# Where eight in-projection weight tiles are split and stored, and when search constants and the first modulation products run

## The chip, the core and the metric

One core of a Trainium2 chip runs the whole program. The metric is the device time of an execution in microseconds. The engines are TensorE (PE: matmuls; PEld: its weight loads), VectorE (DVE), ScalarE (ACT), GpSimd (POOL) and SyncE (SP), whose queue issues nearly all DMAs here. Each engine takes its instructions in a fixed order, and waits on semaphores for the others.

## The reference

One layer of a hybrid decoder trunk on 2048 positions of width 1024, in float32. The input is normalized, scaled and shifted by a modulation vector, projected, and handed to three groups of heads whose outputs are projected back; a gated feed-forward part follows.

```python
mod = c_act @ ada_w[l] + ada_b[l]
sh1, sc1, g1, sh2, sc2, g2 = [m[:, None, :] for m in jnp.split(mod, N_MOD, axis=-1)]
h = rmsnorm(x, norm_mix_w[l]) * (1.0 + sc1) + sh1
proj = h @ w_in[l]
(hq, hf, hi, hg, sq, sk, sv, iq, ik, iw, cu) = jnp.split(proj, offsets, axis=-1)
o_a = hgrn2_mixer(hq, hf, hi, hg, lower_bounds[l], hg_onorm_w[l])
o_b = dsa_mixer(sq, sk, sv, iq, ik, iw)
o_c = conv_module(cu, cv_w[l], cv_b[l], cv_ln_w[l], cv_ln_b[l])
mix = jnp.concatenate([o_a, o_b, o_c], axis=-1) @ w_out[l]
x = x + g1 * mix
h = rmsnorm(x, norm_mlp_w[l]) * (1.0 + sc2) + sh2
x = x + g2 * (jnp.square(jax.nn.relu(h @ mlp_w1[l])) @ mlp_w2[l])
```

`hgrn2_mixer` is a gated linear recurrence in chunks; `dsa_mixer` scores keys with a light indexer (`iq`, `ik`, `iw`), keeps the best 256 keys of each query and attends to them; `conv_module` is a causal depthwise convolution with gating and a layer norm.

## The kernel before, in words

**Precision.** Every large product is made of three: an operand is split into a high part (a cast to fp32r) and a low part (what the cast left over), and high by high, high by low and low by high are summed. So each weight tile is split once: ScalarE casts the high part (`split_w`, L317), GpSimd subtracts the low part (L318), in two halves of 128 x 512.

**Blocks.** The positions go in four blocks of 512. For each block `in_norm` loads and normalizes `x`, `to_act_steps` makes eight slices (k = 0 to 7) of the transposed, modulated activations, each with a high part `ah` and a low part `al` (L281 to L288), and `in_block` runs 26 units, each a weight tile of the in-projection times the slices (`mm_T` at L424, or `n_part` at L1244 for the wide ones, which take two weight tiles). The first units are the index keys, the two index queries (`iq`), then the first head: `hf`, `hq`, `hi` (two tiles) and `hg`. These are the first eight weight tiles. The low part of slices 1, 4 and 6 is made by VectorE, that of the others by GpSimd (L288). Of the first block the first two units run slice by slice as the slices come (`first_units`), in two PSUM tiles called `at`; the third unit is the second index query.

**Weights, once from the input and then split.** The first block fetches each tile raw (512 KB, `fetch_w`, tiles `wraw`, two buffers), splits it, uses it, and then stores both parts (1 MB in four transfers) in a DRAM tile `wk_d` (`keep_w`). The later blocks fetch both parts from there (`fetch_kept`, tiles `wk`). `specs` is the list of all weight tiles in the order of use; an entry of it is raw (its pieces, and a name such as "win", whose names in `keep` are stored) or a kept one (`kept` and its number). Kept weights use the buffers of `whi` and `wlo`, and every third one those of `wraw`, by a counter over the whole program (`w_tiles`).

**Modulation.** Scale and shift for the first slices come first: `ada_half` multiplies 32 loaded tiles `adw` of 128 x 512 by the activated `c`, most on VectorE (L238, L240), some on ScalarE with a sum on GpSimd (L233, L236), sums over the partitions by small matmuls (L226), and writes `a` and `sh` (L244). The rest of the modulation, the gates and the second norm's scale and shift, is made by `ada_gen` from the second block on, in chunks of 256 columns by `ada_part` (L197, L199).

**Constants.** `late_consts` is called in the first block ahead of its second unit. It holds `search_consts` (powers, reciprocals and products of 14 columns, L472 to L491, from which the search for the 256th score starts), the convolution's taps, the recurrence's bounds and five masks `lmask`, each of two selects on GpSimd (L514, L516) and a cast on VectorE (L518).

**What sets the order.** The program's text is not the order of the instructions: a scheduler with a model of time places each instruction on its engine's queue as soon as the model has its inputs ready and the engine free, so what is written late can stand early. `high_priority` moves a few; nothing in the kernel before fixes the place of one instruction behind another beyond that. Background work (index scores, the search for the top 256, attention, convolution, recurrence, `ada`) is written in turns between the units by `step` and `half`.

Of the kernel before, what the change touches and what calls it, by code (L numbers as in the profile page):

```python
# [8 lines left out]
F32 = mybir.dt.float32  # L9
# [11 lines left out]
P = 128  # L21
# [25 lines left out]
PREP = 14  # L47
R1 = [1126, 1216, 1594]
# [30 lines left out]
def trunk(ctx, tc, x, c, ada_w, ada_b, norm_mix_w, norm_mlp_w, w_in, hg_lb_logits,  # L79
# [61 lines left out]
    def dram(shape, dt, name):  # L141
        return tc.dram_tile(shape, dt, name=name)
# [49 lines left out]
    def ada_part(pool, wtag, wbufs, acc, sec, c0, w):  # L192
        for k in range(NK):
            t = pool.tile([P, w], F32, tag=wtag, bufs=wbufs, name=nm("adw"))
            (nc.gpsimd if AQ else nc.sync).dma_start(t, ada2[k * P:(k + 1) * P, sec * D + c0:sec * D + c0 + w])
            if k == 0:
                V.tensor_scalar(acc, t, cact[:, 0:1], None, op0=OP.mult)  # L197
            else:
                V.scalar_tensor_tensor(acc, t, cact[:, k:k + 1], acc, op0=OP.mult, op1=OP.add)  # L199
            yield 1.2 * w  # L200
# [73 lines left out]

    def to_act_steps(xh, acol, bcol, ah, al, mid=None):
        for k in range(NK):
# [11 lines left out]
            (V if k in (1, 4, 6) else G).tensor_tensor(lo, tf, hi.bitcast(F32), OP.subtract)  # L288
# [40 lines left out]
    kept = []  # L329
# [74 lines left out]
    def keep_w():  # L404

        for w, sp in given:
            if sp is not None and sp[1] in keep:
                d = dram([P, 2, TB * 2], F32, f"wk_d{len(kept)}")
                kept.append(d)
                for s_, ts in enumerate(w):  # L410
                    for n, t in enumerate(ts):
                        dma(d[:, s_, n * TB:(n + 1) * TB], raw32(t).rearrange("p k m -> p (k m)"))
        given.clear()
# [343 lines left out]
    def ada_gen():  # L757
        for sec, dst in ((2, None), (4, a2), (3, sh2), (5, None)):
            for c0 in range(0, D, AW):
                acc = hp.tile([P, AW], F32, tag="ada", bufs=1, name=nm("adacc"))  # L760
                yield from ada_part(hp, "adw", AB, acc, sec, c0, AW)
# [319 lines left out]
    def in_block(b, xts, nxt):  # L1081
        act = first_units(xts) if b == 0 else to_act(xts, a1, sh1, lambda: pump("fast", rates["fast"]))
        for u, (pieces, ev, m) in enumerate(in_units):
# [6 lines left out]
            if u == 1 and b == 0:  # L1090
                late_consts()
# [73 lines left out]
    forms = [(kk, m) for _, _, kk, m in specs]  # L1165
    for b in range(1, NB):
        specs += [(kept, i, kk, m) for i, (kk, m) in enumerate(forms)]

    where = {}

    def kept_specs(key, new):

        if key not in where:
            where[key] = len(forms) + sum(len(v[1]) for v in where.values()), new
            return new
        first, old = where[key]
        return [(kept, first + i, *(sp[2:] or (NK, P))) for i, sp in enumerate(old)]
# [476 lines left out]
```

## Time and profile before

| What | us |
|---|---|
| median of 3 runs | 2881.52 |
| lowest and highest run | 2874.92, 2886.61 |
| the profiled execution | 2886.42 |
| its span, first to last instruction | 2884.7 |
| TensorE busy in the span | 2756.2 |
| VectorE, ScalarE, GpSimd busy | 1681.3, 1239.3, 1083.3 |

The profile is of one execution. Matmuls are pipelined, so the records of two of them overlap, and TensorE counts as busy also where its matmuls run at half the clock; how fast they follow one another is seen in the distance of their starts. In rows of the timeline the first number is the start in us from the span's start, the second how long the row's instructions took together, `x8` how many there are, and in brackets the idle time of the engine ahead of the row with what ended it. In rows of groups stand the count, the busy time, the mean in ns, and the idle time ahead. The first block runs from 0 to about 245 us, the second to about 500.

### The profile page before, as it was taken

The page shows a single profiled execution, that of the slowest core. Times are in us where ns is not written, and L with a number is a line of the kernel's source. Part 1 is how long each engine was busy: PE and PEld are TensorE (multiplying, and loading weights), DVE is VectorE, ACT ScalarE, POOL GpSimd, SP SyncE. Part 2 cuts the span into 40 slices and gives each one's busy share as a digit, 9 for nine tenths or more (in the row PEclk, how much of TensorE's full clock was granted, in tenths as well). Part 3 has the DMA queues.
Part 4 walks back from the last instruction along what each step waited for, and adds up shares of the span by engine and source line. Part 5 has one row for each costly group of instructions (what it writes and reads, how often), then busy time and mean ns, then how long its engine had stood idle before and what let it go on. Part 6 is the DMA issues. An engine that isn't in the chain of part 4 may idle for free.

```text
span 2884.7 us, 42781 instructions
## 1 busy us (share of the span) xinstructions
PE 2756.2 (96%) x14116; PEld 2299.5 (80%) x14116; DVE 1681.3 (58%) x3514; ACT 1239.3 (43%) x2630; POOL 1083.3 (38%) x1051
## 2 busy tenths in 40 slices
PE   6999998999999989999999999999999999999997
PEld 5888887888788777888778888787788887777776
DVE  6695687877466447665767637476762221254455
ACT  4436444533311255555455454354543332343333
POOL 7444111212100455666564222134422223345444
PEclk9999999999999999999999999999999999999999
DMA  8987676667655668989888776778867676686676
GB/s 292 293 278 242 214 229 192 215 216 251 207 179 168 228 228 273 307 280 284 279 268 303 231 229 200 217 234 261 281 217 235 205 230 197 219 285 211 227 238 207
DMA packets 428067, 688.55 MB, mean 239 GB/s; under 512 B 43383, under 2 KB 171452, under 8 KB 427836
## 3 DMA queue, kind: packets, MB, share of 16 engines
q1 hardware_dynamic: 427680, 685.67, 73.5%
q8 instruction: 112, 1.84, 0.3%
q14 instruction: 119, 0.97, 0.1%
q10 hardware_dynamic: 156, 0.07, 0.0%
HBM read 532.74 MB, written 152.84 MB: 238 GB/s over the span
## 4 chain that ended last, share of the span: by engine, by line
PE 41%; DMA 6%; DVE 3%; POOL 1%; issue 1%; ACT 0%; SPq 0%; POOLq 0%; DVEq 0%; ACTq 0%
PE mm L1268 11%; PE ax L424 9%; PE mm L424 6%; PE ax L1268 5%; PE mm L1429 4%; PE at L929 1%; PE po L963 1%; DMA wk<-wk_d 1%; PE at L951 1%; DMA tr<-in_mlp_w_dram 1%; PE ix L809 1%; POOL wk L376 1%; DVE cum L881 1%; DMA x_d<-x 1%; DMA wk_d<-whi 1%
## 5 line engine op out<-in xcount | busy, mean ns | idle before, releaser
L424 PE MATMUL mm<-ah,wk 128*128 128x512 f32 x1728 | 461.0, 398 | 4.9 <-ACT tf L286 1.9
L424 PEld LDWEIGHTS mm<-ah,wk 128*128 128x128 f32 x1728 | 319.5, 189 | 71.1 <-ACT tf L286 2.1
L318 POOL TENSOR_TENSOR wlo<-wraw,whi 128x512 fp32r<-128x512 f32 x210 | 288.4, 1395 | 219.9 <-ACT whi L317 137.5
L961 POOL TENSOR_TENSOR pT<-L,pT 128x512 fp32r<-128x512 f32 (+3 forms) x160 | 191.0, 1195 | 387.6 <-ACT pT L960 212.1
L816 DVE SCALAR_TENSOR_TENSOR s<-r,iw_s,s 128x512 f32<-128x512 f32 (+3 forms) x266 | 236.3, 888 | 115.0 <-ACT r L811 108.4
L424 PE MATMUL mm<-al,wk 128*128 128x512 f32 x864 | 237.4, 396 | 0.0
L424 PE MATMUL ax<-ah,wk 128*128 128x512 f32 x912 | 234.5, 391 | 1.4 <-ACT hc L1403 1.4
L1268 PE MATMUL mm<-wk,hh 128*128 128x512 f32 x736 | 224.3, 396 | 3.9 <-DMA wk<-wk_d 3.5
L931 DVE CUSTOM_DVE_ANT_0 L<-at,bias 128x512 f32<-128x512 f32 (+3 forms) x152 | 93.6, 619 | 189.0 <-PE at L929 133.9
L424 PEld LDWEIGHTS ax<-ah,wk 128*128 128x128 f32 x912 | 169.5, 188 | 36.1 <-ACT hc L1403 1.8
L811 ACT ACTIVATE r<-ix 128x512 f32<-128x512 f32 (+3 forms) x256 | 134.3, 554 | 146.3 <-PE ix L809 112.5
L317 ACT CAST whi<-wraw 128x512 fp32r<-128x512 f32 x210 | 122.0, 619 | 173.0 <-DMA wraw<-in_mlp_w_dram 42.1
L273 POOL TENSOR_TENSOR hl<-hr,hh 128x512 fp32r<-128x512 f32 x96 | 131.1, 1366 | 159.8 <-ACT hh L265 159.6
L424 PEld LDWEIGHTS mm<-al,wk 128*128 128x128 f32 x864 | 161.2, 189 | 32.2
L589 DVE SCALAR_TENSOR_TENSOR cx<-hc,cvc,cx 128x512 f32<-128x512 f32 x232 | 173.8, 749 | 2.0
L881 DVE TENSOR_SCALAR_CACHE_REDUCE cum<-s,ssm 128x384 bf16<-128x384 f32 (+13 forms) x112 | 165.2, 1475 | 8.7 <-POOL s L820 6.8
L1268 PEld LDWEIGHTS mm<-wk,hh 128*128 128x128 f32 x736 | 135.5, 188 | 32.6 <-DMA wk<-wk_d 5.8
L959 ACT COPY L<-at 128x512 f32<-128x512 f32 (+3 forms) x160 | 82.7, 522 | 182.1 <-PE at L951 180.4
L1542 DVE TENSOR_TENSOR acc<-acc,mm 128x512 f32<-128x512 f32 x120 | 81.0, 683 | 125.0 <-PE mm L1268 124.4
L1429 PE MATMUL mm<-wk,hc 128*128 128x512 f32 x588 | 144.9, 392 | 6.8 <-DVE acc L1437 6.7
L945 ACT ACTIVATE L<-L,nmx 128x512 f32<-128x512 f32 (+3 forms) x160 | 103.8, 651 | 80.3 <-DVE nmx L940 79.9
L1429 PEld LDWEIGHTS mm<-wk,hc 128*128 128x128 f32 x588 | 109.5, 188 | 33.8 <-DVE acc L1437 10.5
(368 smaller groups left out, 6128.8 us busy)
## 6 DMA issues: line engine op xcount, KB each, us to landing
wk<-wk_d SPq DMA_DIRECT2D x776, 256.0 KB
wk<-wk_d SPq DMA_DIRECT2D x196, 512.0 KB
wk_d<-whi SPq DMA_DIRECT2D x210, 256.0 KB
wk_d<-wlo SPq DMA_DIRECT2D x210, 256.0 KB
wraw<-in_mlp_w_dram SPq DMA_DIRECT2D x68, 512.0 KB
kc<-sk_d SPq DMA_DIRECT2D x112, 256.0 KB
vc<-v_d SPq DMA_DIRECT2D x112, 256.0 KB
adw<-in_ada_w_dram SPq DMA_DIRECT2D x128, 128.0 KB
```

The source lines that it names most:

```text
L273: e.tensor_tensor(lo[:, i:j], src[:, i:j], hi[:, i:j].bitcast(F32), OP.subtract)
L317: A.copy(hi, src)
L318: G.tensor_tensor(lo, src, hi.bitcast(F32), OP.subtract)
L424: T.matmul(ps, ww[k], aa[k], start=(n == 0 and k0 == 0), stop=(n == len(order) - 1 and k1 == NK))
L589: V.scalar_tensor_tensor(acc if w < TAPS - 1 else total, hc[:, w:w + TB], cvc[:, m, w:w + 1], acc, op0=OP.mult, op1=OP.add)
L811: A.activation(r[:, :w], ps[:, :w], AF.Relu, scale=32.0 ** -0.5)
L816: V.scalar_tensor_tensor(s[:, c0:c0 + w], r[:, :w], iw, s[:, c0:c0 + w], op0=OP.mult, op1=OP.add)
L881: V.tensor_scalar(dump, s, t, -AIM - i * STEP, op0=OP.is_ge, op1=OP.add, accum_out=d)
L945: A.activation(lt[:, :w], lt[:, :w], AF.Exp, bias=nmx, accum_out=sm[:, cb:cb + 1])
L961: G.tensor_tensor(pT[:, :nt, 1], lv, pT[:, :nt, 0].bitcast(F32), OP.subtract)
L1268: T.matmul(ps, aa[f][:, tok * P:(tok + 1) * P], ww[i], start=(first and n == 0), stop=(last and n == 5))
L1429: T.matmul(bank[t], aa[:, k, t * P:(t + 1) * P], ww[k], start=(i in (0, 2, 4) and n == 0), stop=(n == 5), skip_group_check=True)
```

## The change

Two things are changed. **The weights:** the first eight tiles are used by the first block as before but not stored ("once" is no name in `keep`). The second block fetches these eight raw again, splits them, and stores them; the third and fourth fetch them from there. `numbers` keeps each kept tile's number as it was. Nothing else about a tile's use changes. **The order:** `lows` collects the low slices' instructions in the order written. `late_consts` stands under an edge behind the eighth (`lows[NK - 1]`, the first block's slice 7, on GpSimd), and the first chunk of `ada_gen` behind the seventh (`lows[NK - 2]`, the first block's slice 6, on VectorE). Such an edge orders only instructions on that same engine: GpSimd's instructions of `late_consts`, and VectorE's products of the first 256 columns of the first gate. DMAs and other engines are held only through what they read.

```diff
+LATE = 8
...
-    def ada_part(pool, wtag, wbufs, acc, sec, c0, w):
+    def ada_part(pool, wtag, wbufs, acc, sec, c0, w, behind=None):
...
-            if k == 0:
-                V.tensor_scalar(acc, t, cact[:, 0:1], None, op0=OP.mult)
-            else:
-                V.scalar_tensor_tensor(acc, t, cact[:, k:k + 1], acc, op0=OP.mult, op1=OP.add)
+            with tc.issue_after(behind) if behind is not None else ExitStack():
+                if k == 0:
+                    V.tensor_scalar(acc, t, cact[:, 0:1], None, op0=OP.mult)
+                else:
+                    V.scalar_tensor_tensor(acc, t, cact[:, k:k + 1], acc, op0=OP.mult, op1=OP.add)
...
+    lows = []
...
-            (V if k in (1, 4, 6) else G).tensor_tensor(lo, tf, hi.bitcast(F32), OP.subtract)
+            lows.append((V if k in (1, 4, 6) else G).tensor_tensor(lo, tf, hi.bitcast(F32), OP.subtract))
...
-    kept = []
+    kept = {}
+    numbers = []
...
-                d = dram([P, 2, TB * 2], F32, f"wk_d{len(kept)}")
-                kept.append(d)
+                i = numbers.pop(0) if numbers else len(kept)
+                kept[i] = d = dram([P, 2, TB * 2], F32, f"wk_d{i}")
...
-                yield from ada_part(hp, "adw", AB, acc, sec, c0, AW)
+                yield from ada_part(hp, "adw", AB, acc, sec, c0, AW, lows[NK - 2].ins if (sec, c0) == (2, 0) else None)
...
             if u == 1 and b == 0:
-                late_consts()
+                with tc.issue_after(lows[NK - 1].ins):
+                    late_consts()
...
+    raws = specs[:LATE]
+    specs[:LATE] = [(sp[0], "once", *sp[2:]) for sp in raws]
+    firsts = len(specs)
     for b in range(1, NB):
         specs += [(kept, i, kk, m) for i, (kk, m) in enumerate(forms)]
+    specs[firsts:firsts + LATE] = raws
...
+    numbers += [*range(LATE, len(forms)), *range(LATE)]
...
+            numbers.extend(range(where[key][0], where[key][0] + len(new)))
```

Since the scheduler's model sees other inputs ready at other times, the order changes on all engines and in most of the program. Three places are shown. Lines of the changed kernel are 1 to 12 above those before (L288 becomes L292, L318 L322, L479 L484).

GpSimd's queue from the first block's last modulation sum on, before. `al` is a slice's low part, `wlo` a weight's, `sconst` the search constants, `rs` the norm of the next block's `x`:

```order
L236 TENSOR_TENSOR adw_469<-adw_469,adw_472 128x512
L288 TENSOR_TENSOR al_368<-tf_369,ah_367 128x512
L479 TENSOR_TENSOR sconst<-sconst 128x14
L480 TENSOR_TENSOR sconst<-sconst 128x14
L318 TENSOR_TENSOR wlo_407<-wraw_373,whi_406 128x512
L318 TENSOR_TENSOR wlo_411<-wraw_373,whi_410 128x512
L288 TENSOR_TENSOR al_517<-tf_518,ah_516 128x512
L288 TENSOR_TENSOR al_539<-tf_540,ah_538 128x512
```

The same place now, as far as the fourth unit's weight (`wraw_404`):

```order
L322 TENSOR_TENSOR wlo_411<-wraw_373,whi_410 128x512
L292 TENSOR_TENSOR al_517<-tf_518,ah_516 128x512
L292 TENSOR_TENSOR al_539<-tf_540,ah_538 128x512
L477 IOTA sint 128x14
...
L519 AFFINE_SELECT mwork<-mwork 128x256
L256 TENSOR_SCALAR rs_2265<-ss_2263 128x1
...
L484 TENSOR_TENSOR sconst<-sconst 128x14
L485 TENSOR_TENSOR sconst<-sconst 128x14
...
L521 AFFINE_SELECT mwork<-mwork 128x256
L257 TENSOR_TENSOR rs_2265<-rs_2265,nhalf 128x1
...
L257 TENSOR_TENSOR rs_2274<-rs_2274,nhalf 128x1
L322 TENSOR_TENSOR wlo_644<-wraw_404,whi_643 128x512
```

The two powers (`sconst`) have moved from ahead of the sixth slice's low part to behind the eighth's, and stand with two mask selects and the norms ahead of the fourth unit's low weights; the other mask selects, which stood among the first 34 rows, follow further on.

VectorE's queue from `al_528`, the seventh low slice, to the low part `slo` of the second index query, now; `adacc` is the first chunk of `ada_gen`, `kst` the index keys:

```order
L292 TENSOR_TENSOR al_528<-tf_529,ah_527 128x512
L199 TENSOR_SCALAR adacc_3685<-adw_3686,cact 128x256
L201 SCALAR_TENSOR_TENSOR adacc_3685<-adw_3713,cact,adacc_3685 128x256
...
L478 CAST sconst<-sint 128x14
...
L201 SCALAR_TENSOR_TENSOR adacc_3685<-adw_3841,cact,adacc_3685 128x256
...
L201 SCALAR_TENSOR_TENSOR adacc_3685<-adw_4038,cact,adacc_3685 128x256
L488 RECIPROCAL sconst<-sconst 128x14
L530 TENSOR_TENSOR kst_570<-stg_568,kst_570 32x512
L543 TENSOR_TENSOR slo_636<-at_414,shi_635 128x512
L486 TENSOR_TENSOR zq<-sconst 128x14
...
L492 TENSOR_TENSOR sconst<-sconst 128x14
L543 TENSOR_TENSOR slo_677<-mm_651,shi_676 128x512
```

Before, the chunk's first four products and the constants down to the one that is now L492 stood ahead of `al_528`, among the slices; only the chunk's last four stood behind it. SP's queue at the same place now, with the loads of the index products (`ki`, `qi`) and of the raw weights of `hi`:

```order
L108 DMA iq_d_75<-slo_636 128x512
L108 DMA ki_729<-ki_d_87 96x384
L108 DMA iq_d_75<-shi_676 128x512
L108 DMA iq_d_75<-slo_677 128x512
L108 DMA qi_724<-iq_d_75 32x8x128 x3
L108 DMA wraw_682<-in_w_in_dram 128x4x256
L108 DMA wraw_751<-in_w_in_dram 128x4x256
```

and TensorE's, where these products are used:

```order
L429 MATMUL mm_761<-al_528,whi_688 128x512
L429 MATMUL mm_761<-al_539,whi_688 128x512
L814 MATMUL at_731<-ki_729,qi_724 128x384
L814 MATMUL at_736<-ki_729,qi_724 128x384
L429 MATMUL mm_692<-ah_334,wlo_644 128x512
```

Before, the first index product stood behind all products of `hi`, and the low half of each unit directly behind its high half; now two index products stand between the high halves of the fourth and fifth unit (`mm_692`, `mm_761`) and their low halves.

GpSimd's queue around the start of the second block, now; before, it had no `wlo` here:

```order
L322 TENSOR_TENSOR wlo_2888<-wraw_2783,whi_2887 128x512
L966 TENSOR_TENSOR pT_2732<-L_2719,pT_2732 128x3x128
L322 TENSOR_TENSOR wlo_3140<-wraw_2881,whi_3139 128x512
...
L322 TENSOR_TENSOR wlo_3144<-wraw_2881,whi_3143 128x512
...
L292 TENSOR_TENSOR al_3024<-tf_3025,ah_3023 128x512
...
L292 TENSOR_TENSOR al_3123<-tf_3124,ah_3122 128x512
...
L322 TENSOR_TENSOR wlo_3286<-wraw_3137,whi_3285 128x512
...
L322 TENSOR_TENSOR wlo_3290<-wraw_3137,whi_3289 128x512
...
L322 TENSOR_TENSOR wlo_3536<-wraw_3283,whi_3535 128x512
```

The first two tiles are split ahead of the second block's slices (`al_3024` is the first), the third and the following ones behind them.

## The prediction

> **What bounds the kernel now.** I read the page's busy table first, then busy time by stage, then single engines in order of time through the first 110 us and at the first block boundary.
>
> ```profile
> span 2884.7 us, 42781 instructions
> PE 2756.2 (96%) x14116; PEld 2299.5 (80%) x14116; DVE 1681.3 (58%) x3514; ACT 1239.3 (43%) x2630; POOL 1083.3 (38%) x1051
> ```
>
> TensorE's queue sets the time; what it doesn't spend on matmuls is 128 us of the span. So the change can pay only where TensorE waits, or runs at its slow clock. By stage (the stretch and its length; busy us and counts of TensorE, its weight loads, VectorE, ScalarE and GpSimd; granted clock, DMA share, GB/s; the row from 190 is from a finer cut):
>
> ```profile
> 20.00:60.00 40.00, 28.47 (x124) 23.83 (x123) 34.01 (x56) 15.85 (x26) 28.92 (x21) 0.96 0.94 303
> 100.00:240.00 140.00, 139.50 (x809) 120.68 (x808) 124.99 (x321) 59.13 (x130) 62.05 (x55) 1.00 0.90 284
> 190.00:210.00 20.00, 19.50 (x122) 17.34 (x121) 20.00 (x45) 5.26 (x10) 8.31 (x7) 1.00 0.88 279
> 240.00:260.00 20.00, 17.87 (x98) 15.88 (x97) 11.75 (x31) 16.95 (x33) 9.85 (x12) 0.74 0.43 138
> 260.00:300.00 40.00, 40.00 (x246) 34.11 (x244) 17.90 (x44) 19.36 (x51) 12.31 (x21) 1.00 0.68 217
> 480.00:520.00 40.00, 31.50 (x158) 25.57 (x158) 37.53 (x106) 24.08 (x52) 12.64 (x16) 0.87 0.45 149
> ```
>
> From 20 to 60 us TensorE is idle 11.5 of 40 us beside VectorE at 34 and GpSimd at 29: that is where the first slices are made. From 100 to 240 us it idles 0.5 of 140 us although DMA stands at 0.90: the stores cost the matmuls nothing there. At the boundaries to the second and third block (240 to 260, 480 to 520) it idles 2.1 and 8.5 us at clocks of 0.74 and 0.87.
>
> **The change, part by part.** First the search constants, held behind the first block's eighth low slice. GpSimd, then ScalarE, then TensorE, before the change:
>
> ```profile
> 48.96 2.60 POOL L479 TENSOR_TENSOR sconst<-sconst 128x14 f32<-128x14 f32 x1 [2.77 <-PE at L424]
> 51.53 2.59 POOL L480 TENSOR_TENSOR sconst<-sconst 128x14 f32<-128x14 f32 x1
> 54.09 2.54 POOL L318 TENSOR_TENSOR wlo<-wraw,whi 128x512 fp32r<-128x512 f32 x2
> 56.58 1.30 POOL L288 TENSOR_TENSOR al<-tf,ah 128x512 fp32r<-128x512 f32 x1
> 60.40 1.29 POOL L288 TENSOR_TENSOR al<-tf,ah 128x512 fp32r<-128x512 f32 x1 [2.52 <-ACT ah L287]
> ...
> 54.42 0.62 ACT L287 CAST ah<-tf 128x512 fp32r<-128x512 f32 x1
> 58.90 0.78 ACT L286 ACTIVATE tf<-mm,sh,a 128x512 f32<-128x512 f32 x1 [3.86 <-DVE gq__210 L488]
> ...
> 60.38 0.50 PE L424 MATMUL mm<-ah,whi 128*128 128x512 f32 x1 [2.69 <-ACT ah L287]
> 62.03 0.63 PE L424 MATMUL at<-al,whi 128*128 128x512 f32 x1
> 62.46 0.63 PE L424 MATMUL at<-ah,wlo 128*128 128x512 f32 x1
> 66.66 0.39 PE L424 MATMUL at<-al,whi 128*128 128x512 f32 x1
> 66.88 0.39 PE L424 MATMUL at<-ah,wlo 128*128 128x512 f32 x1
> ```
>
> Two powers on 14 columns take 5.2 us of GpSimd in front of a weight split and of the sixth slice's low part (56.58). `tf` has two buffers, so the eighth slice's `tf` (58.90) can't begin before that low part is done; ScalarE idles 3.86 us. With the powers behind the slices the 2.54 us split runs from about 49, the low part follows its own cast, and the eighth `tf` can follow the cast at 54.42 directly: **3.9 us** earlier. (Lower end 2.7, TensorE's own wait.) The half clock after that wait, seven steps of 0.43 instead of 0.22 us from 62.03 on, is 1.5 us; a wait elsewhere may bring it back, so I take **1.0** of 0 to 1.5.
>
> Second, the masks and the modulation products, which now stand behind the slices on GpSimd and VectorE. VectorE, then GpSimd beside it:
>
> ```profile
> 27.61 0.29 DVE L518 CAST lmask<-mwork 128x256 uint8<-128x256 f32 x1 [0.54 <-POOL mwork L516]
> 31.23 1.36 DVE L518 CAST lmask<-mwork 128x256 uint8<-128x256 f32 x1 [0.54 <-POOL mwork L516]
> 32.51 5.10 DVE L240 SCALAR_TENSOR_TENSOR adacc<-adw,cact,adacc 128x512 f32<-128x512 f32 x3
> 39.22 0.74 DVE L240 SCALAR_TENSOR_TENSOR adacc<-adw,cact,adacc 128x512 f32<-128x512 f32 x1
> 47.45 0.35 DVE L197 TENSOR_SCALAR adacc<-adw,cact 128x256 f32<-128x256 f32 x1
> 50.58 0.16 DVE L244 TENSOR_TENSOR sh<-ax,cols 128x4 f32<-128x4 f32 x1 [1.14 <-PE ax L226]
> ...
> 4.36 2.13 POOL L516 TENSOR_SCALAR_AFFINE_SELECT mwork<-mwork 128x256 f32<-128x256 f32 x1
> 30.68 0.51 POOL L516 TENSOR_SCALAR_AFFINE_SELECT mwork<-mwork 128x256 f32<-128x256 f32 x1
> 31.17 4.23 POOL L318 TENSOR_TENSOR wlo<-wraw,whi 128x512 fp32r<-128x512 f32 x3
> ```
>
> The second half of the slices waits for `sh` at 50.58, which ends VectorE's series of products. Out of that series go 0.54 + 0.29 + 0.54 + 1.36 + 0.35 = 3.08 us. Between 1 (if loads or the GpSimd series are late next) and 3.1 I take **3.0**, as all of it stands between two products. The products run at 1.70 us each beside GpSimd's split (5.10 for three) and at 0.74 without; that split stays, so its cost stays.
>
> [...]
>
> Third, what is queued behind the moved work. Held, GpSimd's powers, masks and the next block's norms stand ahead of the fourth weight's split. On VectorE the constants that need the powers, and two rounds of modulation products that need fresh loads, stand ahead of the second index query's low part; SP's queue stands still at that store, with the `qi` load and the next raw weights behind it. And TensorE's order now has two index products (`at` from `ki` and `qi`) ahead of the fourth and fifth unit's low halves.
>
> ```profile
> 69.60 1.98 PE L424 MATMUL mm<-ah,whi 128*128 128x512 f32 x8
> 71.42 1.52 PE L424 MATMUL mm<-al,whi 128*128 128x512 f32 x6
> 72.78 0.60 PE L529 MATMUL ax<-ident,stg 128*128 128x128 f32 x4
> ...
> 60.23 1.05 ACT L259 ACTIVATE xdump<-xt 128x1024 bf16<-128x1024 f32 x1
> 77.52 0.32 SPq L107 DMA_DIRECT2D iq_d<-slo  x1
> 83.83 2.00 SPq L107 DMA_DIRECT2D qi<-iq_d  x3
> 94.06 0.51 PE L809 MATMUL at<-ki,qi 96*128 96x384 f32 x2
> ```
>
> Before, `qi` is asked for 6.3 us after the store and used 10 us later: ample. After, count from the end of the eighth cast. ScalarE has four norms (1.05 each, and a read-out) and eight copies and casts of about 0.6 up to and with the query's high part: some 9.6 us; its low part makes 10.3. Store to `qi` is at most 6.3 and, without the weight stores between, perhaps 3; the loads then take about 2. So `qi` lands 15.3 to 18.6 us after the cast. TensorE gets the low slice after 1.3 us and then has 4 products of it, 15 of the third unit, 16 of the fourth and 16 of the fifth: 51 at 0.23 (eight in the 1.82 us from 69.60 to 71.42) are 11.7, and transposes 0.9 (four take 0.60): 13.9 in all. It waits 1.4 to 4.7 us; I take **2.0** lost, near the short end, since the stores that stretched the 6.3 are gone.
>
> [...] Here 2.69 us of waiting already ended at 0.43 us steps. Were it to strike at `qi` too, that is the second rival.
>
> Fourth, eight tiles of weights stored by the second block. The first block no longer writes 8 x 1 MB; the second reads 0.5 instead of 1 MB each and writes them.
>
> ```profile
> 23.61 10.10 SPq L107 DMA_DIRECT2D adw<-in_ada_w_dram  x16
> 34.12 1.66 SPq L107 DMA_DIRECT2D wk_d<-whi  x3
> L318 POOL TENSOR_TENSOR wlo<-wraw,whi 128x512 fp32r<-128x512 f32 x210 | 288.4, 1395 | 219.9 <-ACT whi L317 137.5
> L317 ACT CAST whi<-wraw 128x512 fp32r<-128x512 f32 x210 | 122.0, 619 | 173.0 <-DMA wraw<-in_mlp_w_dram 42.1
> ```
>
> The first stores are issued at 34.12, behind the last loads for the slices; nothing of the slices waited for them: 0 in the first block, up to 1 gained. In the second block 16 casts (16 x 0.62 = 9.9 us of ScalarE) and 16 splits (16 x 1.40 = 22.3 us of GpSimd) are new. Between 260 and 300 ScalarE is busy 19.4 and GpSimd 12.3 of 40 us, and the first two tiles' casts stand ahead of the slices, in the first block's end. I take 0, from -1 to +6. Four MB more in some 50 us is 80 GB/s on a stage at 217, below the 284 that hindered nothing.
>
> **Sum:** -3.9 - 1.0 - 3.0 + 2.0 + 0 = -5.9 us. The profiled execution took 2886.42 us, 4.9 above the median of 2881.52; it would become 2880.5, and the median **2875.5**. With every term at its better end it is -3.9 - 1.5 - 3.1 + 1.4 - 1 = -8.1, at its worse end -2.7 - 0 - 1 + 4.7 + 6 = +7.0. The order of every engine changes later too, with the same matmuls: I allow 6 us either way.
>
> **Rivals.** (1) *Not kept.* From 190 to 210 us VectorE is busy 20 of 20 us. If it and not TensorE sets the first block's end, an earlier TensorE only meets it, and ten selects of 0.5 to 2.1 us, some 13 in all, now run beside it after 60 us: what was freed is paid back. Against: TensorE's idle 0.5 us in 140. Time: about 2881.5.
>
> (2) *The `qi` wait at full length, with the clock.* 4.7 us, and 1.5 for the half clock again, against 7.9 gained: -1.7, 2880.
>
> (3) *Slower: GpSimd sets the second block's first eight units.* They are 8 x 24 x 0.23 = 44 us of matmuls. GpSimd has 12.3/40 of that, 13.5 us, and 22.3 new: 35.8. From about 1.2 times its alone durations (beside VectorE they reach 1.7) it is full, and each tile waits for its own two splits, 8 x 2.8 = 22 us; less 5.9, 16 lost: 2898. For: those slices at 240 are already short of ScalarE (16.95 of 20). Against: the first block lives with splits in every unit and TensorE idles 0.5 us in 140.
>
> (4) *More.* The terms at their better ends (8.1), and the reordered boundary at 480 to 520, idle 8.5 us, closing by most of it (7): 2866.4. For: that order is new on every engine. Against: nothing in the change aims there.
>
> That the change doesn't do what it says is excluded for the order; only instructions on the named slice's engine are held, the modulation loads are not.
>
> **Numbers.** Forecast 0.47 (2868 to 2882); rivals 1 and 2 0.19 (2878 to 2886); 3 0.10 (2886 to 2900); 4 0.24 (2856 to 2868). The range 2860 to 2889 leaves out the far part of 3 and of 4. 0.5% is 14.4 us, about what a measurement tells from no change: faster, below 2867.1, is nearly all of 4: 0.23; slower, above 2895.9, half of 3: 0.05; same 0.72.
>
> **What would show it.** Right: the eighth low slice ends near 55 instead of 61.7 us; no 2.6 us powers before it; `sh` near 47.5; TensorE's wait at the first index product about 2 us; 100 to 240 still near 0.5 us idle. Wrong: waits at the fourth to seventh unit for `wlo` or `qi`; waits for `wlo` between 245 and 300; the first block ending where it did, or a boundary that moved by more than 6 us.

## The result and the profile after

| What | Before | After |
|---|---|---|
| median, us | 2875.83 (7 runs) | 2896.22 (7 runs) |
| lowest and highest run | 2871.58, 2886.61 | 2891.09, 2901.11 |
| span of the profiled execution | 2884.7 | 2894.3 |
| TensorE busy in the span | 2756.2 | 2762.5 |

The two medians alone would give 1.0071; the ratio of the runs, which is used from here on, is 1.0058, with an interval of 1.0043 to 1.0072. So the change costs about 17 us, where a gain of 6 was forecast.

The busy table of the changed kernel, then its busy time by stage. The rows read as those before (engines in the order TensorE, its weight loads, VectorE, ScalarE, GpSimd; granted clock, DMA share, GB/s):

```profile
PE 2762.5 (95%) x14116; PEld 2303.1 (80%) x14116; DVE 1683.9 (58%) x3514; ACT 1251.7 (43%) x2646; POOL 1109.7 (38%) x1067
```

```profile
20.00:60.00 40.00, 32.49 (x140) 27.79 (x141) 29.49 (x41) 21.62 (x36) 24.33 (x20) 0.91 0.79 257
60.00:90.00 30.00, 25.04 (x132) 21.42 (x131) 22.68 (x42) 13.34 (x26) 26.00 (x22) 0.94 0.44 133
100.00:240.00 140.00, 140.00 (x811) 121.07 (x810) 112.91 (x293) 56.78 (x122) 60.92 (x56) 1.00 0.88 267
240.00:260.00 20.00, 14.02 (x87) 11.43 (x86) 14.53 (x35) 17.84 (x32) 13.41 (x13) 0.91 0.65 214
260.00:300.00 40.00, 40.00 (x239) 33.90 (x238) 18.86 (x41) 28.31 (x61) 25.99 (x29) 1.00 0.90 293
480.00:520.00 40.00, 32.39 (x162) 26.23 (x160) 35.28 (x89) 25.24 (x56) 14.88 (x18) 0.87 0.50 166
1525.00:1565.00 40.00, 35.30 (x166) 28.60 (x165) 31.70 (x51) 24.22 (x53) 21.08 (x19) 0.91 0.75 244
2830.00:2860.00 30.00, 25.97 (x120) 22.30 (x120) 12.08 (x14) 8.27 (x14) 14.98 (x13) 0.89 0.67 215
```

The kernel before in those of the stretches that were not shown of it:

```profile
60.00:90.00 30.00, 29.62 (x159) 25.68 (x160) 13.40 (x21) 16.57 (x30) 16.48 (x18) 0.94 0.90 303
1525.00:1565.00 40.00, 39.45 (x192) 32.78 (x192) 34.82 (x61) 25.52 (x53) 17.85 (x18) 1.00 0.92 325
2830.00:2860.00 30.00, 29.87 (x186) 26.77 (x185) 18.87 (x23) 11.90 (x26) 17.05 (x13) 1.00 0.79 261
```

From 20 to 60 us TensorE gains 4 us of busy time, as was meant. From 60 to 90 it loses 4.6 again. The stages of which the prediction was afraid are sound: 140.00 of 140 in the first block, 40.00 of 40 at 260 to 300, where the eight tiles are split. Between them, from 240 to 260 us, TensorE is busy 3.9 us less (14.02 for 17.87), at a higher granted clock (0.91 for 0.74). And two stretches far from the change, near 1550 us and at the end, lose 4 us each and their full clock.

**The start.** GpSimd, VectorE's `sh`, and ScalarE, after the change:

```profile
54.09 1.32 POOL L292 TENSOR_TENSOR al<-tf,ah 128x512 fp32r<-128x512 f32 x1 [1.79 <-ACT ah L291]
58.55 2.60 POOL L484 TENSOR_TENSOR sconst<-sconst 128x14 f32<-128x14 f32 x1 [0.31 <-DVE sconst L481]
64.07 2.15 POOL L521 TENSOR_SCALAR_AFFINE_SELECT mwork<-mwork 128x256 f32<-128x256 f32 x1
67.63 5.92 POOL L322 TENSOR_TENSOR wlo<-wraw,whi 128x512 fp32r<-128x512 f32 x4
76.78 3.34 POOL L322 TENSOR_TENSOR wlo<-wraw,whi 128x512 fp32r<-128x512 f32 x2
...
48.22 0.16 DVE L246 TENSOR_TENSOR sh<-ax,cols 128x4 f32<-128x4 f32 x1 [1.69 <-PE ax L228]
...
70.65 9.87 SPq L108 DMA_DIRECT2D wraw<-in_w_in_dram  x3
```

The eighth low slice ends at 55.4 us instead of 61.7. But the powers and selects now stand ahead of the splits, which begin at 67.63: by the rows, two end near 70.6, four at 73.55, six at 80.12. A raw buffer is free when its tile is split, and SP's three loads of the next raw weights are issued from 70.65 on and stretch over 9.87 us. TensorE, with the waits in brackets:

```profile
71.94 0.58 PE L814 MATMUL at<-ki,qi 96*128 96x384 f32 x2 [0.70 <-DMA qi<-iq_d]
78.00 0.74 PE L1256 MATMUL mm<-whi,ah 128*128 128x256 f32 x4 [1.47 <-ACT k L639]
82.61 0.73 PE L1256 MATMUL mm<-whi,ah 128*128 128x256 f32 x4 [2.80 <-DVE q L648]
83.65 1.04 PE L1256 MATMUL mm<-wlo,ah 128*128 128x256 f32 x4
90.30 0.64 PE L1256 MATMUL mm<-whi,ah 128*128 128x256 f32 x4
94.38 0.64 PE L1256 MATMUL mm<-wlo,ah 128*128 128x256 f32 x4
```

and ScalarE and VectorE ahead of the two waits at `hi`:

```profile
74.41 1.14 ACT L321 CAST whi<-wraw 128x512 fp32r<-128x512 f32 x2 [1.14 <-DMA wraw<-in_w_in_dram]
75.57 1.28 ACT L636 ACT_TABLE_LOAD   x1
77.35 0.59 ACT L639 ACTIVATE k<-mm 128x512 f32<-128x512 f32 x1
...
78.36 2.18 DVE L821 SCALAR_TENSOR_TENSOR s<-r,iw_s,s 128x384 f32<-128x384 f32 x2 [1.01 <-ACT r L816]
80.47 1.49 DVE L640 TENSOR_SCALAR f<-f 128x512 f32<-128x512 f32 x1
81.88 0.67 DVE L648 SCALAR_TENSOR_TENSOR q<-mm,u 128x512 f32<-128x512 f32 x1
```

The wait for `qi` is 0.70 us. The next ends with `k`, which frees a PSUM bank and stands on ScalarE behind a cast that waited for the raw weights, and behind a table load of 1.28 us; before, the same table load ran from 74.02 on, and ScalarE still idled 0.84 us behind it. The third wait ends with `q`, which stands on VectorE behind index sums that weren't there before. Then TensorE is at half clock (granted 0.51 from 83.6 to 87.1 us), four products of 256 columns in 1.04 us instead of 0.64 (at 90.30). There are 16, from 83.65 to 87.06: 3.41 us instead of 16 x 0.12, 1.5 lost. In all 0.70 + 1.47 + 2.80 + 1.5 = 6.5 us. The last products of `hi`, at 94.38, stood here before:

```profile
92.42 0.64 PE L1244 MATMUL mm<-wlo,ah 128*128 128x256 f32 x4
```

Eight index products have passed ahead of them, about 0.18 us each by the starts, 1.4 of the 2 us. At TensorE the start had gained 6.7 us (the third unit's last eight products begin at 61.06 instead of 67.79); it is gone by 95 us, and what makes the kernel slower must lie behind.

### The profile page after: what moved, and what is told of

Read it like the earlier page. It is cut to its first block, busy times and chain, and to the rows that moved or that the text cites. A ratio compares the mean times of both kernels' runs of the same rounds, so it can differ in the third digit from the quotient of the medians.

```text
span 2894.3 us, 42818 instructions
## 1 busy us (share of the span) xinstructions
PE 2762.5 (95%) x14116; PEld 2303.1 (80%) x14116; DVE 1683.9 (58%) x3514; ACT 1251.7 (43%) x2646; POOL 1109.7 (38%) x1067
## 4 chain that ended last, share of the span: by engine, by line
PE 43%; DMA 6%; DVE 4%; issue 1%; POOL 1%; ACT 0%; SPq 0%; POOLq 0%; DVEq 0%; ACTq 0%
PE mm L1280 11%; PE ax L429 10%; PE mm L429 7%; PE ax L1280 5%; PE mm L1441 3%; DMA wk<-wk_d 2%; PE po L968 2%; PE at L934 2%; PE at L956 1%; PE ix L814 1%; DMA tr<-in_mlp_w_dram 1%; POOL wk L381 1%; DVE cum L886 1%; DMA kc<-sk_d 1%; DVE s L821 1%
## 5 line engine op out<-in xcount | busy, mean ns | idle before, releaser
L429 PE MATMUL mm<-ah,wk 128*128 128x512 f32 x1632 | 435.2, 398 | 3.3 <-ACT tf L290 1.5
L322 POOL TENSOR_TENSOR wlo<-wraw,whi 128x512 fp32r<-128x512 f32 x226 | 310.5, 1395 | 222.4 <-ACT whi L321 127.7
L429 PEld LDWEIGHTS mm<-ah,wk 128*128 128x128 f32 x1632 | 303.1, 190 | 66.7 <-issue 1.7
L429 PE MATMUL mm<-al,wk 128*128 128x512 f32 x816 | 225.1, 397 | 0.0
L321 ACT CAST whi<-wraw 128x512 fp32r<-128x512 f32 x226 | 132.0, 620 | 181.0 <-PE mm L429 40.2
L429 PEld LDWEIGHTS mm<-al,wk 128*128 128x128 f32 x816 | 152.9, 190 | 30.3
```

The costliest lines, as they stand in the source:

```text
L321: A.copy(hi, src)
L322: G.tensor_tensor(lo, src, hi.bitcast(F32), OP.subtract)
L429: T.matmul(ps, ww[k], aa[k], start=(n == 0 and k0 == 0), stop=(n == len(order) - 1 and k1 == NK))
```

## The experiments

Three theories. **A:** the work held back is met again between 60 and 90 us, and takes the start's gain back; the rest is the changed order. **B:** splitting and storing eight tiles in the second block costs the time. **C:** the counter that gives out the weight buffers is shifted, and other tiles in the raw buffers cost the time, wherever that is.

Each ratio is to the kernel before, run on the same chip, with its 95% interval; 0.1% is 2.9 us. The sets of runs of the kernel before that go with the experiments had medians of 2878.9 to 2882.6 us.

### The two parts apart

First the edges without the weights, then the weights without the edges.

```diff
-LATE = 8
+LATE = 0
```

> Both edges, no weight moved (LATE = 0). Theory A (the work held back meets the first block a second time, as waits on raw weights and on qi between 70 and 85 us, and the rest is a reshuffle): the start gains about 6 us at the eighth low slice and gives most of it back; ratio to before 0.998 to 1.001, and TensorE's waits of 0.9, 1.6 and 3.0 us at 70 to 82 us are seen here too. Theory B (splitting and storing eight weight tiles in the second block costs the time): the edges alone are the gain forecast, 0.997 to 0.998. Theory C (any shift of the order, through the weight buffers' every-third turn, moves the time by some 10 us): 0.996 to 1.004, not to be told beforehand.

```diff
-                yield from ada_part(hp, "adw", AB, acc, sec, c0, AW, lows[NK - 2].ins if (sec, c0) == (2, 0) else None)
+                yield from ada_part(hp, "adw", AB, acc, sec, c0, AW, None)
...
-                with tc.issue_after(lows[NK - 1].ins):
-                    late_consts()
+                late_consts()
```

> Eight tiles stored by the second block, no edges. Theory A: the start is that of before (eighth low slice at 61 to 62 us) with none of the waits at 70 to 82 us; ratio to before 1.003 to 1.005, below the changed kernel's 1.0058, because what remains is the reshuffle alone. Theory B: 1.006 to 1.009, above the changed kernel, as the start's gain is missing too. Theory C: slower than before by 1.003 to 1.006, since the buffers' turn is shifted by eight tiles as in the changed kernel.

Measured: edges 1.0026 (1.0010 to 1.0042), weights 1.0075 (1.0048 to 1.0101). The edges alone are slower than theory A or B has them: the eighth low slice ends at 54.7 us, but from 60 to 90 us TensorE is busy 25.60 of 30. The weights alone cost more than the whole change, with 30.00 of 30 there. So the loss between 60 and 90 belongs to the edges, and most of the 17 us to the weights. Theory A had put the weights below the changed kernel, and missed; theory C's 1.003 to 1.006 lies below them too, though their interval reaches into it, and only theory B's 1.006 to 1.009 holds them. For the edges theory C had named only a wide range (0.996 to 1.004).

### The buffers' turn alone

The first eight tiles of the second block are now fetched raw, and `fetch_w` doesn't count in `w_tiles`. So from its ninth tile on, the counter that gives every third kept tile the buffers of `wraw` stands eight lower, and other tiles get them, to the end of the program. Eight lower is as one higher, modulo three. This is tried in the kernel before, where nothing else is touched, and put back in the changed one:

```diff
-    turn = [0]
+    turn = [1]
```

and in the changed kernel, and in that with the weights alone (`weights_turn`):

```diff
-    turn = [0]
+    turn = [2]
```

> The kernel before with the counter that gives every third kept tile the raw buffers started at 1 instead of 0: from the second block on the turn is that of the changed kernel; no work is added, removed or held. Theories A and B: 1.000 within 0.0015. Theory C: 1.003 to 1.006.

> The changed kernel with that counter started at 2, so that from the ninth tile of the second block on the turn is that of before. Theories A and B: the changed kernel's 1.006 within 0.0015. Theory C: 1.000 to 1.003, the time of the changed kernel less what the shifted turn cost.

> The eight weight tiles stored by the second block, no edges, with the counter of the buffers' turn started at 2 (before's turn from the ninth tile of the second block on). If the turn is what the moved weights cost, 1.000 to 1.002, since without it eight more splits in the second block hide (theory C). If the splits themselves cost (theory B), 1.003 to 1.006 with waits at 240 to 300 us.

Measured:

| | turn shifted | turn as before |
|---|---|---|
| kernel before | 1.0033 (1.0019 to 1.0047) | 1 |
| weights, no edges | 1.0075 (1.0048 to 1.0101) | 1.0038 (1.0023 to 1.0052) |
| both (the change) | 1.0058 (1.0043 to 1.0072) | 1.0018 (1.0001 to 1.0035) |

Three times the shift costs 0.33 to 0.40%, 10 to 12 us, without one instruction more. Theory C holds for the turn, but not for the weights: it left 1.000 to 1.002 for the moved weights with the turn as before, and they cost 1.0038, theory B's range. In that run TensorE waits among the products of `hi` in the second block:

```profile
300.98 0.39 PE L968 MATMUL po<-pT,vc 128*128 128x256 f32 x1 [1.34 <-POOL pT L966]
303.38 0.92 PE L676 MATMUL ax<-q,k 128*128 128x192 f32 x4 [1.90 <-DVE r L756]
```

It waits for steps of attention (`pT`) and recurrence (`r`) that share ScalarE and GpSimd there with the casts and splits of the moved tiles (two casts of 0.63 and 0.60 us from 295.99 on, two splits of 1.28 and 1.27 us from 296.69 on, the second directly ahead of `pT`). These are 3.2 us, and the granted clock is 0.83 from 300 to 310 us, where the kernel before has 1.00; counted by the columns that TensorE has worked off, summed over its products as a measure of the work done, this run loses 5.5 us to the kernel before between 287 and 313 us. The loss was 0.38%, some 11 us; where the rest lies, and how much of all this the moved splits make, stays open. In the changed kernel TensorE is busy 40.00 of 40 us in that stage, and with both edges whole the moved weights cost nothing that can be told: 1.0018 with them, 1.0026 without. That isn't so with the smaller edges further below.

### Where the turn costs

In the changed kernel the counter is moved on by 2 ahead of the last feed-forward part, then ahead of the first; in the kernel before it is moved on by 1 for the last part alone, and for the first part alone.

That of tail_turn (mlp_turn has the step ahead of the loop, tail_only adds 1 in the kernel before), and that of mid_only:

```diff
     for b in range(NB):
+        if b == NB - 1:
+            turn[0] += 2
         for ev in mlp_block(b):
```

```diff
     for b in range(NB):
+        if b < 2:
+            turn[0] += 1 + b
         for ev in mlp_block(b):
```

> The changed kernel with the counter moved on by 2 ahead of the last block's feed-forward part, so that only there the turn is that of before. Theory C (the turn decides which kept tile sits in a raw buffer when the last four raw tiles are wanted): the wait of 4 us for the first of them near 2849 us goes, and the time is 4 to 7 us below the changed kernel's: ratio to before 1.003 to 1.005; the waits near 1545 to 1558 us stay. Rival (the tail is a matter of the order alone, not of the buffers): the wait stays in some form, 1.005 to 1.007.

> The changed kernel with the counter moved on by 2 ahead of the first block's feed-forward part, at about 600 us, so that the in-projections keep the changed kernel's turn and all feed-forward parts have that of before. Theory C: both waits of the shifted turn, 8.5 us near 1550 us and 6 us near 2849 us, go, and some 5 us that it gained near 1950 us are lost: 1.001 to 1.003 against 1.0058. Rival (the turn matters through the in-projection's blocks and their order): 1.004 to 1.007.

> The kernel before with the counter moved on by 1 ahead of the last block's feed-forward part: everything up to about 2400 us is as before, after it the turn is the changed kernel's. Theory C: the wait for the first of the last four raw tiles, 4 to 7 us at the end, appears, with nothing else; ratio to before 1.001 to 1.0025. Rival (the tail's wait is met by a gain elsewhere, as the small difference of the run with only the tail's turn put back suggests): 0.999 to 1.001.

> The kernel before with the counter moved on by 1 ahead of the first block's feed-forward part and by 2 more ahead of the second's: only the first block's feed-forward part has the changed kernel's turn. Theory C: the waits of 8 to 9 us at its end, near 1550 us, appear, with what the same turn does before that from 650 us on; ratio 1.002 to 1.004. Rival: the waits there need the whole shifted order; 0.999 to 1.001.

Measured: tail_turn 1.0051 (1.0035 to 1.0066), mlp_turn 1.0042 (1.0027 to 1.0056), tail_only 1.0029 (1.0015 to 1.0043), mid_only 1.0032 (1.0018 to 1.0046). Rows of these stretches, first of mlp_turn, then of tail_only, then of mid_only:

```profile
1525.00:1565.00 40.00, 39.27 (x193) 32.69 (x192) 36.50 (x70) 25.35 (x53) 18.81 (x17) 1.00 0.89 311
2830.00:2860.00 30.00, 29.52 (x188) 26.75 (x187) 19.16 (x23) 11.10 (x25) 16.80 (x13) 1.00 0.79 258
```

```profile
2830.00:2860.00 30.00, 26.00 (x145) 23.39 (x144) 14.92 (x17) 7.24 (x12) 14.57 (x11) 0.89 0.71 239
```

```profile
1525.00:1565.00 40.00, 36.72 (x176) 29.96 (x175) 29.65 (x43) 22.22 (x51) 19.19 (x19) 0.96 0.96 328
```

Each loss comes and goes with the turn of its own feed-forward part: with tail_turn TensorE is busy 35.54 of 40 us in the first stretch and 30.00 of 30 in the second, with the turn alone shifted (phase_only) 34.15 and 25.97, and with the change and the old turn (both_phase) 39.48 and 29.84. In mid_only the loss near 1550 us is 2.7 us, smaller than the 4.2 of the change. The mechanism at the end is seen on SP and TensorE, after the change and then before:

```profile
2833.64 4.88 SPq L108 DMA_DIRECT2D wk<-wk_d  x4
2848.60 0.93 SPq L108 DMA_DIRECT2D wraw<-in_mlp_w_dram  x2
...
2846.14 2.88 PE L1441 MATMUL mm<-wk,hc 128*128 128x512 f32 x12
2853.05 0.79 PE L1256 MATMUL ax<-whi,hh 128*128 128x256 f32 x2 [4.03 <-ACT whi L321]
```

```profile
2838.42 0.38 SPq L107 DMA_DIRECT2D wraw<-in_mlp_w_dram  x1
2844.71 0.40 SPq L107 DMA_DIRECT2D wraw<-in_mlp_w_dram  x1
...
2845.48 0.52 PE L1244 MATMUL ax<-whi,hh 128*128 128x256 f32 x3
```

The last four weight tiles are raw, and need the two `wraw` buffers. Before, the first load is issued 7 us ahead of the products that need it. After the change a kept tile holds both buffers until the last of the products begun at 2846.14; the loads are issued at 2848.60, and TensorE idles 4.03 us and goes on at half clock (granted 0.50 from 2853 to 2858 us; eight products of 256 columns in 1.91 us from 2855.48 on). Near 1550 us the way is longer. VectorE after, with the product of TensorE that ends it, then VectorE before:

```profile
1552.77 4.71 DVE L1566 TENSOR_TENSOR acc<-acc,gb 128x1024 f32<-128x1024 f32 x3 [3.60 <-DMA gb<-g_d]
1557.40 0.34 DVE L821 SCALAR_TENSOR_TENSOR s<-r,iw_s,s 128x128 f32<-128x128 f32 x1
...
1558.11 0.40 PE L814 MATMUL ix<-ki,qi 96*128 96x128 f32 x1 [2.34 <-ACT r L816]
```

```profile
1544.24 5.45 DVE L1554 TENSOR_TENSOR acc<-acc,gb 128x1024 f32<-128x1024 f32 x4
...
1558.62 0.27 DVE L814 TENSOR_SCALAR s<-r,iw_s 128x128 f32<-128x128 f32 x1
```

With the shifted turn the scheduler has put the block's end (`acc` by the gate `gb`) between two index sums of 128 columns, the first at 1548.77. It waits 3.60 us for its load, the second sum waits behind it, ScalarE's next `r` for the sum, and TensorE 2.34 us for that. Before, `acc` found its load there, and the sums of that width came behind it, from 1558.62 on.

Of mlp_turn the trace gains more than the runs do: its profiled execution was one of its quickest (2887.53 us; median 2894.0). Theory C's 1.001 to 1.003 missed, and its 1.0042 lies in the range of the rival, by which the turn matters through the in-projections, which keep the shifted turn here (1.004 to 1.007). So part of the turn's cost may lie there; no run moves the in-projections' turn alone. tail_turn, 1.0051, lies just above theory C's range and inside its rival's, though the wait that the rival kept is gone; its converse, tail_only, decides for the end: 0.29%, 8 us (4 to 12), more than the 1.001 to 1.0025 expected.

The two places don't make up the account. Alone they cost 0.29 and 0.32%, and the whole shift, with both, costs 0.33% (each give or take 0.14). Counted by the columns that TensorE has worked off, the trace of phase_only loses 12 to 14 us to the two traces of the kernel before between 1420 and 1600 us and about 7 from 2690 us on, and gains 9 to 14 between 1935 and 2690 us. So the shift changes the order in many places, for better and worse; the two are those where it loses most.

The third turn, `turn = [2]` in the kernel before, and the changed kernel once more:

> The kernel before with the counter started at 2: the third of the three turns. If the kernel before stands at a turn that was picked among three for its time, this one costs as the one shifted by 1 did, 1.002 to 1.004; if the shift by 1 is a bad turn of itself, 0.999 to 1.001.

> The changed kernel once more, unchanged, on the same chip as the three others, for a second profile and more runs. All theories: 1.0045 to 1.007, with the waits at 70 to 82, 1545 to 1558 and 2849 us in their places.

Measured: 1.0023 (1.0009 to 1.0037), and 1.0065 (1.0047 to 1.0084). So the kernel before stands at the best of its three turns, and either shift costs it 7 to 10 us.

### What the start can keep

If the held powers and masks are the backlog between 60 and 90 us, less of it should keep the start's gain. So only the two powers are held, with and without the moved weights (there with `turn = [2]`); then without the edge on the modulation products; then the powers behind the splits of the sixth unit's first weight tile, with `search_consts` called at that unit and no longer in `late_consts`.

The powers held, in powers_edges (`LATE = 0`) and powers_late (`LATE = 8`, `turn = [2]`); powers_alone also has `None` for the edge in `ada_gen`:

```diff
-                with tc.issue_after(lows[NK - 1].ins):
-                    late_consts()
+                late_consts()
...
-        G.tensor_tensor(a_, p_, na, OP.pow)
-        G.tensor_tensor(b_, q_, na, OP.pow)
+        with tc.issue_after(lows[NK - 1].ins):
+            G.tensor_tensor(a_, p_, na, OP.pow)
+            G.tensor_tensor(b_, q_, na, OP.pow)
```

powers_later, `LATE = 0` and without that edge too (`splits` collects GpSimd's instructions of `split_w`):

```diff
+        with tc.issue_after(splits[-1]):
+            G.tensor_tensor(a_, p_, na, OP.pow)
+            G.tensor_tensor(b_, q_, na, OP.pow)
...
+            if u == 5 and b == 0:
+                search_consts()
```

> Only the two GpSimd powers wait for the eighth low slice; the ten mask selects run early again; the modulation edge stays; no weight moved. Theory A (the held GpSimd work, powers and masks, delays the weight splits behind it, and so the raw loads of the units at 70 to 82 us): without some 7 us of selects in that stretch TensorE's waits of 1.0, 1.2, 2.3 and 0.6 us shrink to at most 2 us in all, the first 50 us of matmul work end about 3 us earlier than with both edges whole, and the ratio to before is 0.997 to 1.001 against 1.0026. Rival (the waits come from TensorE being early as such, the splits being bound by the raw weights' two buffers): the waits stay within 1 us of what they were, whatever stands on GpSimd; 1.002 to 1.004.

> The same, with the eight weight tiles stored by the second block and the counter of the buffers' turn started at 2, as in the run that had both parts and before's turn. Theory A: the waits at 70 to 82 us, 0.9, 1.5 and 3.1 us there, shrink to 2 us in all; ratio to before 0.997 to 1.000. Rival: the waits stay; 1.001 to 1.003.

> Only the two GpSimd powers wait for the eighth low slice; no edge on the modulation products, no weight moved. If the modulation edge is what made room (the third term of the sum, minus 3 us), the scale and shift come no earlier than in the kernel before (sh at 50.4 to 50.6 us) and the low half of the second index query, in front of which the held products stood, is earlier: TensorE's wait of 2.0 us at 71 us falls to under 1. Then 0.996 to 0.999. Rival: without that edge the products stand between the low slices again, the eighth comes 1 to 2 us later than 56.5 to 57.8, and the ratio is 0.998 to 1.001.

> The two powers wait for the split of the weight tile of the sixth unit instead (about 70 to 75 us), with no other edge and no weight moved. Theory A: GpSimd then has nothing but norms between the slices and the splits, the raw loads come 5 us earlier than with the powers ahead of them, and no wait over 1 us is left between 60 and 90 us; the first 50 us of matmul work end 4 to 6 us before those of the kernel before; ratio 0.995 to 0.999. Rival (waits stay, of TensorE being early as such): 0.998 to 1.001 with a wait of 2 us or more at 70 to 82 us.

| | ratio | last low slice ends | `sh` | TensorE busy, 60 to 90 us |
|---|---|---|---|---|
| before | 1 | 61.7 | 50.58 | 29.62 |
| both edges whole | 1.0026 (1.0010 to 1.0042) | 54.7 | 47.49 | 25.60 |
| powers_edges | 0.9979 (0.9965 to 0.9993) | 57.8 | 50.60 | 28.16 |
| powers_alone | 0.9975 (0.9960 to 0.9990) | 58.3 | 51.06 | 30.00 |
| powers_later | 1.0000 (0.9985 to 1.0015) | 57.3 | 50.10 | 27.15 |
| powers_late | 1.0012 (1.0000 to 1.0023) | 57.0 | 49.83 | 27.20 |

powers_alone and powers_edges beat both kernels. With the masks back in the first 31 us and no products held (powers_alone), TensorE waits for nothing from 60 to 90 us, and the end of `hi` is kept 3.8 us ahead of the 92.42 before:

```profile
88.58 0.64 PE L1256 MATMUL mm<-wlo,ah 128*128 128x256 f32 x4
```

`sh` is as late as before in both: it was the masks' casts that came out of VectorE's series, and the edge on the modulation products gave nothing that can be told (0.9979 with it, 0.9975 without). powers_later missed, and the figures of its rival came, a wait of over 2 us and 0.998 to 1.001; but the wait has another cause than the rival's, TensorE being early as such. GpSimd was free earlier, but then made the next block's norms, whose products (three of 1.78 us, one of 0.75) stood on VectorE ahead of the `slo` that frees a PSUM bank:

```profile
72.99 2.11 PE L430 MATMUL mm<-ah,whi 128*128 128x512 f32 x8 [2.85 <-DVE slo L544]
```

The moved weights take the gain back here, though the turn is that of before: 1.0012 where 0.997 to 1.000 was expected, against 0.9979 without them. So they cost 0.3 to 0.4% in two of three pairs and nothing in the third. By the columns worked off, powers_late loses some 7 us to powers_edges between 235 and 257 us, at the boundary to the second block: TensorE has waits there for `k`, one of 1.89 us, and granted clocks of 0.73, 0.84 and 0.75 in the three stretches of 10 us from 240 on, where powers_edges has 1.00 in each.

### The kernel before once more

> The kernel before once more, unchanged, for a second profile: how far two executions of one kernel differ, and where. All theories: within 0.4% of the first, the stretches of TensorE's waits at the same places.

One run, 2877.4 us, with a span of 2875.7 where the first profile had 2884.7. The order of the instructions is the same; the 9 us lie in waits a little shorter at many places. So a difference of a few us between two profiles, here 9.6 in the spans of before and after, says little without the timed runs.

## Why the prediction was wrong

Its start was right in the main. The eighth `tf` follows its cast (52.58 us instead of 58.90), and `sh` came 2.4 us earlier for the 3.0 allowed; the eighth low slice came 6.3 us ahead. Three readings were off. What held the eighth `tf` before was not the sixth low part, which ended at 57.88, but VectorE, as the prediction's own row says (`gq`, L488): its seventh low part ended at 58.80, behind constants that need the powers. The powers were the cause either way. At TensorE that term came near its lower end, its own wait of 2.7 us: with the 2.4 and the 1.5 of the clock that is 6.6, against 6.7 measured and 7.9 forecast. And for `sh` the products counted for nothing, only the masks.

**The first step that failed** is the third, what is queued behind the moved work. It asked only for `qi`, and took 2.0 us; `qi` cost 0.70, but the whole came to 6.5. The list of what is queued was written down rightly, GpSimd's splits behind powers, masks and norms, and the next raw weights behind SP; but it was priced by one chain, that of `qi`. Not priced were the raw loads, which wait for the splits; ScalarE's cast, which waits for the loads with `k` behind it; and VectorE's index sums ahead of `q`. "What would show it" named waits for `wlo` or `qi` at the fourth to seventh unit, and these came in another form, at the sixth. That powers_alone, with the masks early and the products not held, has no wait there supports it; the three links weren't tried apart.

**The second, and larger,** is the fourth part with the allowance for the rest: "I take 0, from -1 to +6", and "the order of every engine changes later too, with the same matmuls: I allow 6 us either way". The change's own text moves the counter by eight, and the prediction treated the buffers of the second to fourth block as unmoved; the description's "Nothing else about a tile's use changes" was wrong for this reason. So a term of some 10 us stood at nothing. The turn alone costs 9.5 us (5.5 to 13.5), and putting it back takes the change from 1.0058 to 1.0018. Two places where it loses are known, and the end's loss is a plain wait for a buffer; what it does in between, for better and worse, is not taken apart.

Rival 3, GpSimd setting the second block's first units, didn't come in the changed kernel: GpSimd is busy 26 of 40 us at 260 to 300, and TensorE 40 of 40. Two sums were wrong: 217 and 80 GB/s are 297, above the 284 that "hindered nothing" and not below (293 were measured there, and TensorE still didn't wait), and 2881.5 less 5.9 is 2875.6. The first block kept its pace, so rival 1's reason fell, as the forecast had it; its outcome, what was freed paid back, came all the same, at 70 to 87 us. The boundary at 480 to 520 closed by only 0.9 us of the 7 that rival 4 asked for. The half clock that a wait elsewhere might bring back came, at `hi` (granted 0.51 from 83.6 to 87.1 us).

The terms as measured: start -6.3 at the slice (-6.7 at TensorE), waits and clock at 70 to 87 us +6.5, turn +10 to +12; and with the turn as before both parts together, these waits included, cost 0.18% (0.01 to 0.35), 5 us. What makes these 5 us isn't settled. The edges (1.0026) and the weights (1.0038) don't add up to it; that each changes the order in which the other is placed may be why, but isn't shown.

## What to carry to other kernels

Where buffers are given out by a counter, a change that adds or drops one call moves every later tile to another buffer: run the kernel before with the counter shifted, and start the changed one so that its turn is the old one, before its time is read. When work is held back behind a critical stretch, price all the queues it then stands ahead of, loads and PSUM banks too, and not the first consumer alone; holding only the instruction that blocked (two powers of 2.6 us) gained 0.25%, holding all its neighbours lost 0.26%.

## What the runs showed of the hardware

TensorE's clock didn't follow the length of its wait in the three cases compared here. The same wait near 1545 us, in the changed kernel and in the kernel before with its turn shifted:

```profile
1547.22 0.44 PE L814 MATMUL ix<-ki,qi 96*128 96x128 f32 x2 [1.67 <-DMA ki<-ki_d]
1547.68 1.00 PE L1280 MATMUL mm<-whi,hh 128*128 128x512 f32 x2
1548.48 1.06 PE L1280 MATMUL mm<-whi,hl 128*128 128x512 f32 x2
```

```profile
1542.01 0.44 PE L809 MATMUL ix<-ki,qi 96*128 96x128 f32 x2 [1.54 <-DMA ki<-ki_d]
1542.60 0.73 PE L1268 MATMUL mm<-whi,hh 128*128 128x512 f32 x2
1543.17 0.62 PE L1268 MATMUL mm<-whi,hl 128*128 128x512 f32 x2
```

After 1.67 us two products last 1.06 us, half clock (granted 0.50 from 1548 to 1550); after 1.54 us 0.62, full clock (1.00 from 1542 to 1546, and the four rows that follow last 0.62 too); and after the 2.85 us in powers_later eight last 2.11, full clock too (1.00 from 60 to 90). So a wait of 1.67 us stood ahead of half clock once, and one of 2.85 did not; no run shows what decides. The other surprise is the spread of one kernel, 2866.7 to 2888.7 us over all runs of the kernel before on several chips, 0.8% with the same order of instructions (0.7% among those on one chip, 2866.7 to 2886.5).
